# Neighbourhood attention on one Trainium2 core: its operands split where they are made, and its first loads and the decays put in order

## The chip, the core and the metric

The kernel runs on one core of a Trainium2 chip. The metric is the device time of one execution in microseconds (us). TensorE (PE) multiplies matrices, VectorE (DVE), ScalarE (ACT) and GpSimd (POOL) work on tiles in on-chip memory (SBUF, and PSUM for results of matmuls), and SyncE (SP) and POOL issue the transfers (DMAs) between SBUF and DRAM. Each engine runs its own instructions in order and waits on the others by semaphores.

## The reference

One layer of an encoder on 1024 tokens of width 1024: a half-step SwiGLU feed-forward, token mixing, a second feed-forward. Token mixing is what matters here:

```python
rq, rk, rv, rg, nq, nk, nv, g_ret, g_na = jnp.split(u @ w_in, points, axis=-1)
q = _rotary(heads(rq, RET_QK_DIM), pos)
k = _rotary(heads(rk, RET_QK_DIM), pos) * (RET_QK_DIM ** -0.5)
y = _bidirectional_retention(q, k, heads(rv, RET_V_DIM), decay_fwd, decay_bwd)
...
y_na = _neighborhood_attention(na_heads(nq), na_heads(nk), na_heads(nv), rel_bias) @ w_na_out
merged = jax.nn.sigmoid(g_ret) * y_ret + jax.nn.sigmoid(g_na) * y_na
return merged @ w_out
```

Neighbourhood attention has 8 heads of 64 on a grid of 16 rows by 64 columns. A block of 16 query columns looks at 32 key columns and a window of 8 rows:

```python
qg = (q * (DH ** -0.5)).reshape(B, rows, GRID_W, NH, DH)
s = jnp.einsum('bnqhd,brnkhd->bhnqrk', q_r, k_blk).astype(jnp.float32)
s = jnp.where(col_mask[:, :, None, :], s + bias, NEG_INF)
p = jax.nn.softmax(s.reshape(B, NH, ncb, NA_Q_BLOCK_COLS, kr * NA_K_BLOCK_COLS), axis=-1)
o = jnp.einsum('bhnqrk,brnkhd->bnqhd', p, v_blk)
```

## The kernel before

All products are of float32 accuracy made from matmuls in a shorter format. `Core.split` writes a value as a high part h, a rounded copy by ScalarE, and a low part l = value - h, by VectorE (or POOL where the caller asks for it). `mm3` multiplies with three matmuls: high by high, high by low, low by high. The large projections run as Strassen-like block products: `Pairs.run` (one job is two blocks of 512 output columns) loads two weight tiles `wraw` through SP, makes their sums and differences and splits them (`wh`, `wl`), runs seven products, and puts the four halves of the result together on VectorE (L519 to L545). `done(j)` is called as each half is ready.

The mixing projection makes, in order: the first four value tiles (`vproj` with `done_nv`, L1313), four jobs for the queries and keys of neighbourhood attention, after the fourth of them the other four value tiles and the gather, then retention's jobs: rotary ones, in which `rotate` (L1043, L1044) multiplies with sine and cosine tables, stores the half on POOL (L69), and leaves two accumulating DMAs, the swaps (L1048, L1049), for the next `done`; and jobs with an activation (L1374). Finished halves lie in a ring of six tiles, `ev`; a tile can be written again once the DMAs that read it have landed. The halves go to DRAM: `nq`, `nk`, `nv`, `rq`, `rk` and others. The gather (L1387) is four DMAs of SP from DRAM to DRAM that copy the 32 key columns of each of the four column blocks from `nv` into `nvg`, 1 MB each.

`na_cores` (L868) then runs attention as 32 units: 4 pairs of heads, each with 8 pairs of a row group and a column block. A unit's steps: scores by two matmuls a head (L921; each operand of k holds the high part in 64 partitions and the low part in the other 64), bias and row maximum on VectorE (L922, with L924), exponential on ScalarE (L926), reciprocal (L928) and scaling (L930) on VectorE, six transposes on TensorE (L940), a split of these, nine matmuls with the values, and a copy (L956). Steps of three neighbouring units overlap. Before use, the kernel loads keys (`kraw`, L891), queries (`qraw`, L879) and values (`vraw`, L904) from DRAM and splits them: keys on ScalarE and VectorE, or POOL for some, queries with the factor 1/8 (L65, L66), values on ScalarE and VectorE.

Between the steps `fill` takes matmuls from a generator, `products`, which makes the retention values (`vproj` with `done_rv`) and the gates: 12 steps of it ahead of attention, then two and two per unit. `Decays` (L999 to L1035) computes the decay tables of retention from 8 logits by some 45 operations on tiles of 8 columns; it stands in the program at unit 12.

The order in which instructions stand on an engine is set by a scheduler from their dependences, priorities and estimates, so it may differ from the order in which the code is written. DMAs go through eight semaphore lanes on SP and eight on POOL: a DMA waits for the one eight before it.

## Time and profile before

| | us |
|---|---|
| median of three runs | 2256.87 (2256.64 to 2257.74) |
| profiled execution, its own time | 2259.97 |
| its span, first to last instruction | 2258.2 |
| TensorE busy | 2201.1 (97%) |
| VectorE busy | 1638.7 (73%) |
| ScalarE busy | 984.6 (44%) |
| POOL busy | 581.0 (26%) |

Times in the views are us from the start of the span. The query and key jobs run at about 700 to 790, the gather and the rotary jobs from 811 on, attention from about 1005 to 1210. In a timeline a row has the start, the duration, the engine, the line, the operation and its tiles, and in brackets the time that the engine stood idle before and what released it. `PE ps L921 <- ACT qh L65: 2.6, 1, 2.6` in a list of waits reads: TensorE at line 921 waited for the tile qh that ScalarE wrote at line 65, 2.6 us in all, once, the longest 2.6 us.

### The profile page before, as it was taken

The page shows a single profiled execution, that of the slowest core. Times are in us where ns is not written, and L with a number is a line of the kernel's source. Part 1 is how long each engine was busy: PE and PEld are TensorE (multiplying, and loading weights), DVE is VectorE, ACT ScalarE, POOL GpSimd, SP SyncE. Part 2 cuts the span into 40 slices and gives each one's busy share as a digit, 9 for nine tenths or more (in the row PEclk, how much of TensorE's full clock was granted, in tenths as well). Part 3 has the DMA queues.
Part 4 walks back from the last instruction along what each step waited for, and adds up shares of the span by engine and source line. Part 5 has one row for each costly group of instructions (what it writes and reads, how often), then busy time and mean ns, then how long its engine had stood idle before and what let it go on. Part 6 is the DMA issues. An engine that isn't in the chain of part 4 may idle for free. (4 is left out here: it accounts for less than half of the span.)

```text
span 2258.2 us, 30072 instructions
## 1 busy us (share of the span) xinstructions
PE 2201.1 (97%) x10232; PEld 1828.9 (81%) x10232; DVE 1638.7 (73%) x2911; ACT 984.6 (44%) x2039; POOL 581.0 (26%) x755
## 2 busy tenths in 40 slices
PE   7899999999998999999999999999999999999998
PEld 5688888888786887878888888888887888888886
DVE  7998878765558756769885678553899787876444
ACT  5444434332344322248885675422544343433232
POOL 1121212168521122311101222111112121215942
PEclk9999999999999999999999999999999999999999
DMA  6353434598655564557755467686446443449865
GB/s 251 135 188 144 177 131 173 185 386 295 200 173 177 182 177 130 145 181 236 218 179 175 150 220 234 247 306 227 145 145 213 146 170 137 163 153 365 293 225 179
DMA packets 155240, 449.34 MB, mean 199 GB/s; under 512 B 19600, under 2 KB 50448, under 8 KB 152976
## 3 DMA queue, kind: packets, MB, share of 16 engines
q1 hardware_dynamic: 112656, 311.09, 41.1%
q0 software_dynamic: 42432, 136.35, 16.6%
q8 instruction: 81, 1.33, 0.2%
q14 instruction: 71, 0.58, 0.1%
HBM read 302.66 MB, written 148.90 MB: 200 GB/s over the span
## 5 line engine op out<-in xcount | busy, mean ns | idle before, releaser
L63 DVE TENSOR_TENSOR wl<-wraw,wh 128x512 fp32r<-128x512 f32 x472 | 316.9, 688 | 64.9 <-ACT wh L62 64.6
L62 ACT CAST wh<-wraw 128x512 fp32r<-128x512 f32 x476 | 274.6, 618 | 175.3 <-PE ps L90 63.4
L89 PE MATMUL ps<-wh,g 128*128 128x512 f32 x548 | 214.2, 391 | 0.4 <-DVE tmp L226 0.4
L90 PE MATMUL ps<-wl,g 128*128 128x512 f32 x548 | 213.6, 390 | 0.0
L91 PE MATMUL ps<-wh,g 128*128 128x512 f32 x548 | 213.3, 389 | 0.0
L562 ACT ACTIVATE c<-c 128x512 f32<-128x512 f32 x88 | 55.5, 632 | 194.9 <-DVE c L527 101.0
L63 DVE TENSOR_TENSOR wl<-w,wh 128x512 fp32r<-128x512 f32 x77 | 76.9, 1018 | 87.3 <-ACT wh L62 87.1
L63 DVE TENSOR_TENSOR wl<-x,wh 128x512 fp32r<-128x512 f32 x77 | 78.1, 1030 | 77.5 <-ACT wh L62 76.1
L89 PEld LDWEIGHTS ps<-wh,g 128*128 128x128 f32 x548 | 102.9, 188 | 21.8 <-DVE tmp L226 0.7
L90 PEld LDWEIGHTS ps<-wl,g 128*128 128x128 f32 x548 | 102.9, 188 | 21.5 <-DVE wl L63 0.5
L91 PEld LDWEIGHTS ps<-wh,g 128*128 128x128 f32 x548 | 102.9, 188 | 21.4
L89 PE MATMUL ps<-a11h,wh 128*128 128x512 f32 x276 | 111.0, 402 | 7.9 <-ACT wh L62 7.9
L62 ACT CAST wh<-t 128x512 fp32r<-128x512 f32 x58 | 36.0, 621 | 189.0 <-DVE t L521 188.9
L91 PE MATMUL ps<-a11h,wl 128*128 128x512 f32 x276 | 109.4, 397 | 6.3 <-DVE wl L63 6.1
L89 PE MATMUL ps<-a22h,wh 128*128 128x512 f32 x280 | 109.9, 392 | 0.0
L91 PE MATMUL ps<-a22h,wl 128*128 128x512 f32 x280 | 109.2, 390 | 0.6 <-DVE wl L63 0.6
L90 PE MATMUL ps<-a11l,wh 128*128 128x512 f32 x276 | 109.3, 396 | 0.1
L89 PE MATMUL ps<-a12h,wh 128*128 128x512 f32 x276 | 108.8, 394 | 0.5 <-ACT wh L62 0.3
L90 PE MATMUL ps<-a22l,wh 128*128 128x512 f32 x280 | 109.1, 390 | 0.0
L90 PE MATMUL ps<-a12l,wh 128*128 128x512 f32 x276 | 107.5, 390 | 0.0
L91 PE MATMUL ps<-a12h,wl 128*128 128x512 f32 x276 | 107.5, 389 | 0.0
L89 PE MATMUL ps<-s2h,wh 128*128 128x512 f32 x232 | 92.7, 400 | 7.6 <-ACT wh L62 7.6
(430 smaller groups left out, 6295.7 us busy)
## 6 DMA issues: line engine op xcount, KB each, us to landing
wraw<-in_dram SPq DMA_DIRECT2D x204, 512.0 KB, 4.5
g<-g0s SPq DMA_DIRECT2D x44, 512.0 KB, 4.3
g<-g1s SPq DMA_DIRECT2D x44, 512.0 KB, 5.5
g<-g0a SPq DMA_DIRECT2D x33, 512.0 KB, 3.5
g<-g1a SPq DMA_DIRECT2D x33, 512.0 KB, 4.3
g0s<-gth POOLq DMA_DIRECT2D x44, 256.0 KB, 5.0
g0s<-cmb POOLq DMA_DIRECT2D x44, 256.0 KB, 3.8
g1s<-gth POOLq DMA_DIRECT2D x44, 256.0 KB, 4.4
```

What stands on the lines that cost most here:

```text
L62: self.done = [nc.scalar.copy(h, src).ins, (eng or nc.vector).tensor_tensor(l, src, hf, ALU.subtract).ins]
L63: (eng or nc.vector).tensor_tensor(l, src, hf, ALU.subtract).ins]
L89: mm(ps, a[0], b[0], start=start, stop=False)
L90: mm(ps, a[0], b[1], start=False, stop=False)
L91: mm(ps, a[1], b[0], start=False, stop=stop)
L562: nc.scalar.activation(gate[j], gate[j], AF.Silu)
```

## The change

The split of neighbourhood attention's operands moves from `na_cores` to where they are made. In the four jobs `done` splits each half into two tiles (queries, halves 0 and 1, with their columns ordered by column block; keys, halves 2 and 3; the factor 1/8 goes into the keys), and stores both. `done_nv` does so for the values. The DRAM tensors `nq`, `nk`, `nv` and `nvg` have a high and a low part, the gather is eight DMAs, and `na_cores` loads the parts straight into the operands' tiles: 16 DMAs for keys where there were 4, 64 for queries where there were 16, and 32 for values where there were 16. No matmul is added or taken away.

The order is changed in two places. `after` adds order-only dependences: the load of the third fill weight of `vproj` may not stand ahead of attention's first key and query loads (`qk`), and the first three operations of `Decays` may not stand ahead of the reciprocal of the unit last written before it (`c.mark`).

```diff
+    def after(self, e, names):
+        for n in names:
+            self.tc.add_manual_dep(e, n, mybir.DependencyInfo(
+                mybir.DependencyClass.NoSync, mybir.DependencyReason.DATA), reason="order")
...
-def na_cores(c, pool, d, bias, fill, n0, n1, n2, side={}):
+def na_cores(c, pool, d, bias, fill, n0, n1, n2, side={}, first=None):
...
+    def fetch(t, src):
+        names.append(nc.sync.dma_start(t, src).ins.name)
+
+    def qload(hp, cb):
+        q = pool.tile([P, 2, 2, 256], F32, tag="q", name="q", bufs=3)
+        for half in range(2):
+            for n in range(2):
+                fetch(q[64 * half:64 * half + 64, :, n],
+                      d["nq"][hp, n, cb].rearrange("(e p) r c -> p e (r c)", e=2))
+        qop[hp, cb] = [[q[:, e, n].bitcast(F32R) for n in range(2)] for e in range(2)]
...
     def load(hp):
-        kr = pool.tile([P, S], F32, tag="kraw", name="kraw", bufs=1)
-        nc.sync.dma_start(kr, d["nk"][hp])
-        kop[hp] = [pool.tile([P, S], F32R, tag=f"k{e}", name=f"k{e}", bufs=2) for e in range(2)]
...
+            k = pool.tile([P, S], F32, tag=f"k{hp % 2}{e}", name=f"k{hp % 2}{e}", bufs=1)
+            for n in range(2):
+                r = 64 * (e ^ n)
+                fetch(k[r:r + 64], d["nk"][hp, n, 64 * e:64 * e + 64])
+            kop[hp].append(k.bitcast(F32R))
 
     def vload(hp, cb):
...
-        c.split(vh, vl, vr)
-        vop[hp, cb] = vh, vl
+        v = [pool.tile([P, 4, P], F32, tag=f"v{q}", name=f"v{q}", bufs=3) for q in "hl"]
+        for n in range(2):
+            nc.sync.dma_start(v[n], d["nvg"][n, cb][:, :, hp * P:(hp + 1) * P].rearrange("t p d -> p t d"))
...
-        nc.vector.reciprocal(rc, st[:, 4:6])
+        c.mark = nc.vector.reciprocal(rc, st[:, 4:6]).ins.name
...
     load(0)
-    qload(0)
-    qsplit(0, 0)
+    qload(0, 0)
+    first.extend(names)
     fill(n0)
...
-        nc.vector.tensor_scalar(a, x, -1.0, None, ALU.mult)
+        c.after(nc.vector.tensor_scalar(a, x, -1.0, None, ALU.mult).ins, [c.mark])
...
+                    if k > 3 and qk:
+                        c.after(c.fetch, qk)
+                        qk.clear()
...
     def done_nv(t, b):
-        e = evpool[0].tile([P, 512], F32, tag="ev", name="ev", bufs=6 if len(evpool) == 1 else 4)
-        nc.scalar.copy(e, b)
-        c.store(d["nv"][2 * t:2 * t + 2].rearrange("r c d -> (r c) d"), e)
+        h, l = (evpool[0].tile([P, 512], F32, tag="ev", name="ev", bufs=6 if len(evpool) == 1 else 4) for _ in range(2))
+        c.split(h.bitcast(F32R), l.bitcast(F32R), b)
+        for q, e in enumerate((h, l)):
+            c.store(d["nv"][q, 2 * t:2 * t + 2].rearrange("r c d -> (r c) d"), e)
...
             def done(j):
                 h = j % 2
+                if fn == "na":
+                    a, l = parts[j], half() if j < 2 else parts[j]
+                    hi = half()
+                    if j < 2:
+                        c.split(*[q.bitcast(F32R).rearrange("p (b r c) -> p r b c", b=4, r=8) for q in (hi, l)],
+                                a.rearrange("p (r b c) -> p r b c", b=4, r=8))
+                    else:
+                        c.split(hi.bitcast(F32R), l.bitcast(F32R), a, scale=0.125)
+                    for q, e in enumerate((hi, l)):
...
+                            c.store(g[q][:, h * 512:(h + 1) * 512], e)
+                    return
...
                 for cb in range(4):
-                    nc.sync.dma_start(d["nvg"][cb].rearrange("t (r c) d -> (t r) c d", r=4),
-                                      d["nv"][:, KEY_OFF[cb]:KEY_OFF[cb] + 32, :])
+                    for q in range(2):
+                        nc.sync.dma_start(d["nvg"][q, cb].rearrange("t (r c) d -> (t r) c d", r=4),
+                                          d["nv"][q, :, KEY_OFF[cb]:KEY_OFF[cb] + 32, :])
```

How the instructions stand after the change is shown at three places. The first is SP from the gather (`nvg<-nv`) to attention's first loads; `decx`, `dectb` and `decd` are tables of the decays, `bt` the bias, `rg` a part of retention. Before:

```order
L1387 DMA nvg<-nv 16x16384 x4
L73 DMA wraw<-in_dram 128x1024 x21
L999 DMA decx<-in_dram 128x8
L1018 DMA dectb<-in_dram 128x4
L1020 DMA decd<-in_dram 128x256
L73 DMA wraw<-in_dram 128x1024
L1144 DMA rg<-rg 128x2x128 x2
L891 DMA kraw<-nk 128x1024
L879 DMA qraw<-nq 64x1024 x4
```

With the change:

```order
L1408 DMA nvg<-nv 16x16384 x8
L73 DMA wraw<-in_dram 128x1024 x16
L997 DMA decx<-in_dram 128x8
L1016 DMA dectb<-in_dram 128x4
L1018 DMA decd<-in_dram 128x256
L1142 DMA rg<-rg 128x2x128 x2
L881 DMA k_8444<-nk 64x1024 x2
L881 DMA k_8447<-nk 64x1024 x2
L881 DMA q<-nq 64x2x256 x4
L911 DMA bt<-in_dram 128x768
L881 DMA q<-nq 64x2x256 x4
L73 DMA wraw<-in_dram 128x1024
```

The gather has twice the DMAs, and six weight loads (21 and 1 before, 16 now) stand behind the first key and query loads instead of ahead of them.

The second place is TensorE where attention begins: scores (`L921`), fill matmuls of `vproj` (`wh`, `wl` with `a12h` or `a12l`), the first transposes (`L940`). Before, of the first scores:

```order
L90 MATMUL ps<-wl,a12h 128x512
L921 MATMUL ps<-k_8346,qh 128x384
L91 MATMUL ps<-wh,a12l 128x512
L89 MATMUL ps<-wh,a12h 128x512
L90 MATMUL ps<-wl,a12h 128x512
L91 MATMUL ps<-wh,a12l 128x512
L921 MATMUL ps<-k_8346,ql 128x384
L89 MATMUL ps<-wh,a12h 128x512
```

With the change (lines moved by 5 in `mm3`: L94 to L96):

```order
L96 MATMUL ps<-wh,a11l 128x512
L921 MATMUL ps<-k_8444,q 128x384
L921 MATMUL ps<-k_8447,q 128x384
L921 MATMUL ps<-k_8444,q 128x384
L921 MATMUL ps<-k_8447,q 128x384
L921 MATMUL ps<-k_8444,q 128x384 x2
L921 MATMUL ps<-k_8447,q 128x384 x2
L921 MATMUL ps<-k_8444,q 128x384 x2
L940 MATMUL pt<-ident,s 128x128 x5
L94 MATMUL ps<-wh,a12h 128x512 x3
```

The ten score matmuls now stand in one piece, and right behind them the transposes of the first unit's softmax; the fill that stood among the scores comes after.

On ScalarE the first instruction that needs the exponential's table was the decays' (L1004), ahead of attention. It is now the first unit's:

```order
L1394 ACTIVATE ev<-ev 128x512 x4
L926 ACT_TABLE_LOAD
L926 ACTIVATE s,nast<-s,nast 128x384 x2
L62 CAST wh<-wraw 128x512 x2
L62 CAST pth<-pt 128x384
```

The table load has moved from the operations of the decays to the first softmax.

More of the change, by code (lines that the diff above doesn't have):

```diff
@@ L1008, in __init__ @@
         nc.vector.tensor_tensor(w, z, z, ALU.mult)
-        nc.vector.memset(s, 1.0 / 17.0)
+        c.after(nc.vector.memset(s, 1.0 / 17.0).ins, [c.mark])
         for n in (15, 13, 11, 9, 7, 5, 3, 1):
@@ L1321, in done_rv @@
         return f
-    jobs = [(16 + i, 20 + i, d["nq"][i], d["nk"][i], None) for i in range(NHP)]
+    jobs = [(16 + i, 20 + i, d["nq"][i], d["nk"][i], "na") for i in range(NHP)]
     for i in range(RH):
@@ L1366, in done @@
                 h = j % 2
+                if fn == "na":
[7 more added lines that the diff above has]
+                    for q, e in enumerate((hi, l)):
+                        if j < 2:
+                            c.store(f[q][:, :, 8 * h:8 * h + 8].rearrange("b p r c -> p b (r c)"),
+                                    e.rearrange("p (b x) -> p b x", b=4))
+                        else:
+                            c.store(g[q][:, h * 512:(h + 1) * 512], e)
+                    return
                 dst = (f, g)[j // 2][:, h * 512:(h + 1) * 512]
```

44 lines of the change are left out of this document (14 added, 30 removed).

## The prediction

> **What bounds the kernel now.** I read the page first, then one table of windows, then the waits of TensorE, and last the timelines of the three places that the change touches. The page:
>
> ```profile
> span 2258.2 us, 30072 instructions
> ...
> PE 2201.1 (97%) x10232; PEld 1828.9 (81%) x10232; DVE 1638.7 (73%) x2911; ACT 984.6 (44%) x2039; POOL 581.0 (26%) x755
> ...
> PE 38%; DVE 1%; issue 1%; ACT 0%; POOL 0%; DMA 0%; POOLq 0%; DVEq 0%
> ```
>
> TensorE is busy 2201.1 of 2258.2 us, and the chain that ended last runs almost only over it. The change leaves every matmul in place, so it can only move TensorE's idle time. The windows (columns: window, length, busy us and count of PE, PEld, DVE, ACT, POOL, then granted clock, DMA share, GB/s) say where that idle time is:
>
> ```profile
> 700.00:800.00 100.00, 96.03 (x423) 78.51 (x422) 73.50 (x117) 32.64 (x56) 11.61 (x21) 1.00 0.48 161
> 800.00:900.00 100.00, 97.61 (x424) 80.29 (x423) 63.49 (x99) 27.42 (x49) 25.75 (x38) 0.98 0.59 171
> ...
> 1000.00:1100.00 100.00, 93.97 (x517) 80.66 (x516) 88.36 (x260) 81.40 (x207) 13.71 (x17) 0.98 0.78 245
> 1100.00:1200.00 100.00, 99.12 (x576) 87.24 (x575) 75.48 (x215) 76.37 (x197) 6.50 (x12) 1.00 0.59 189
> ```
>
> The first two windows hold the projection that makes queries, keys and values; the others hold the attention. Attention idles TensorE 100 - 93.97 = 6.0 us in its first window and 0.9 in the next, while VectorE is 88% and ScalarE 81% busy. TensorE's waits from 990 to 1130 name what ended them:
>
> ```profile
> PE ps L921 <- ACT qh L65: 2.6, 1, 2.6
> PE ps L89 <- ACT pth L62: 2.0, 2, 1.6
> PE pt L940 <- DVE ptl L63: 1.3, 2, 0.9
> PE pt L940 <- DVE s L930: 1.0, 2, 0.7
> ```
>
> Together 6.9 us: one wait for the first split query, the rest for the softmax and the split of its transposed result. That 6.9 us of idle is the pool from which the attention half can gain. Matmuls that start late without a named wait may add a little, by my estimate 2 us at most, so I bound the gain there at 9.
>
> **Part one, the splits move into the projection (690 to 810).** Four jobs now do four splits each on halves, one ScalarE and one VectorE operation per half, and the value tiles get eight VectorE subtracts. Rows of the projection:
>
> ```profile
> 727.25 0.69 DVE L530 TENSOR_TENSOR ev<-ps,ev 128x512 f32<-128x512 f32 x1 [1.95 <-PE ps L91]
> 729.96 0.69 DVE L534 TENSOR_TENSOR ev<-ps,ev 128x512 f32<-128x512 f32 x1 [2.03 <-PE ps L91]
> 730.57 0.68 DVE L520 TENSOR_TENSOR wraw<-wraw 128x512 f32<-128x512 f32 x1
> ```
> ```profile
> 715.12 0.50 PE L91 MATMUL ps<-a11h,wl 128*128 128x512 f32 x1 [3.34 <-DVE wl L63]
> ```
> ```profile
> L69 POOL DMA_DIRECT2D nq<-ev x8: 542/542/558, 720.2 to 782.6; - x8
> ```
>
> VectorE starts such operations 0.60 us apart when nothing waits (729.96 to 730.57), so the added work is (16 + 8) x 0.60 = 14.4 us. It waits for TensorE at 727.25 and 729.96 by about 2 us each, and the window leaves it 26.5 us idle of 100, so 16 splits (9.6 us) fit behind matmuls from there on. Ahead of that, the first four value subtracts (2.4 us) fall into the stretch that ends in TensorE's 3.34 us wait at 715.12, where VectorE is the late one. If each delayed TensorE by its whole length, the cost would be 2.4; one that only takes the place of the existing wait costs nothing. I take 1.0 us, range 0 to 2.4. POOL gets 8 more stores for queries, 8 for keys and 8 for values at 0.542 us, 13 us spread over a window in which it is busy 11.6 of 100: nothing. ScalarE, 32.6 of 100 busy, hides its part too.
>
> **Part two, the gather of the values (811 to 845).** SP copies the value rows in DRAM to a gathered layout, four copies now, eight after. What one batch does to the transfers is in the DMA view of 811 to 827 (first row: busy tenths in 40 slices of 0.4 us) and of 817.9 to 825.2, and in the timelines of SP, POOL, DVE and PE, with the usual landing of a half-size swap (median 3.9 us) from the DMA view of 805 to 860:
>
> ```profile
> 811.83 2.45 SPq L1387 DMA_DIRECT2D nvg<-nv  x4
> ```
> ```profile
> DMA  1000099900004940000099000000994000000420
> ...
> q1 hardware_dynamic: 128, 4.19, 76.5%
> ...
> rq<-ev POOLq DMA_DIRECT2D x1, 256.0 KB, 10.0
> nvg<-nv SPq DMA_DIRECT2D x4, 9.7
> ```
> ```profile
> q1 hardware_dynamic: 64, 2.10, 86.2%
> q0 software_dynamic: 32, 0.13, 5.2%
> ```
> ```profile
> 827.53 0.89 POOL L1048 DMA_DIRECT2D rq<-ev  x1 [9.73 <-DMA rq<-ev]
> 828.12 1.15 POOL L1049 DMA_DIRECT2D rq<-ev  x1
> ```
> ```profile
> rq<-ev POOLq DMA_DIRECT2D x6, 128.0 KB, 3.9
> ```
> ```profile
> 832.08 0.69 DVE L1043 TENSOR_TENSOR ev<-ev,tab 128x512 f32<-128x512 f32 x1 [2.87 <-DMA rq<-ev]
> 832.69 0.68 DVE L63 TENSOR_TENSOR wl<-wraw,wh 128x512 fp32r<-128x512 f32 x1
> ```
> ```profile
> 836.30 0.39 PE L91 MATMUL ps<-s1h,wl 128*128 128x512 f32 x1
> ```
>
> The bursts of slices stand 8 slices apart, 3.2 us: each copy is one wave over all 16 engines, four end near 825.3. The 256 KB store of the rotary query, on POOL's queue, took 10.0 us, and in the second view only half of it (32 packets, 0.13 MB) got through while two waves ran: its packets squeeze in between waves, two per engine each time. POOL then waits 9.73 us for it before it issues the two accumulating swaps (L1048, L1049; 3.9 us each when nothing is in the way), and VectorE's L1043 at 832.08 waits 2.87 us for those, because it writes into their ring slot.
>
> After the change the eight copies begin about 2 us later, since the last of eight value stores comes later and the ring of six tiles makes the fourth split wait for the first store. They end at 814 + 8 x 3.2 = about 840. The store itself still gets its halves through by about 828. But the swaps, issued there, now stand among four more waves: each is half the store, so it too needs two turns, and two swaps need four turns of 3.2 us. They land near 841 and not before 832. L1043 would start about 9 to 10 us later, and the split behind it on VectorE (832.69) with it; its result is used at 836.30, which leaves 836.30 - 833.37 = 2.9 us of slack. TensorE therefore idles 10 - 2.9 = about 7 us. Range: 0, if the swaps get through as soon as the waves thin, to 9.
>
> The Trainium skill has a rule that speaks against this price: DMA: Bandwidth & Descriptors, section "Queues, rings and completion order", says that each DMA engine takes turns between queue rows a whole packet at a time, and that a packet typically holds some 9 to 17 descriptors, which would put a swap's share of one engine into a single turn. The second view does not agree, since half of the store needed a turn of its own; by the rule the swaps would land near 834 and cost TensorE nothing, which is the first rival below.
>
> **Part three, attention (1000 to 1210).** Removed, from the groups of the two windows on VectorE:
>
> ```profile
> L66 DVE SCALAR_TENSOR_TENSOR ql<-qraw,qh 128x256 fp32r<-128x256 f32 x32 | 14.1, 454 | 0.0
> L63 DVE TENSOR_TENSOR vl<-vraw,vh 128x512 fp32r<-128x512 f32 x16 | 11.0, 689 | 1.4 <-ACT vh L62 1.1
> L63 DVE TENSOR_TENSOR k<-kraw,k 64x512 fp32r<-64x512 f32 x10 | 7.7, 784 | 2.2 <-ACT k L62 2.0
> ```
>
> That is 32.8 us off VectorE and about as much off ScalarE. It is not TensorE's time: only the 6.9 us above can come back. The first wait (2.6, for the query) goes, because queries and keys are now fetched before the third fill weight and need no split. What is late next is the softmax of the first unit, since TensorE's order now has no fill between scores and transposes:
>
> ```profile
> 1000.63 0.39 PE L89 MATMUL ps<-wh,a11h 128*128 128x512 f32 x1
> ...
> 1008.79 0.39 PE L89 MATMUL ps<-wh,a12h 128*128 128x512 f32 x1
> ...
> 1020.87 0.34 PE L921 MATMUL ps<-k,qh 128*128 128x384 f32 x1
> 1021.05 0.34 PE L921 MATMUL ps<-k,ql 128*128 128x384 f32 x1
> ```
> ```profile
> 1003.55 1.28 ACT L1004 ACT_TABLE_LOAD   x1
> ...
> 1020.92 0.61 ACT L926 ACTIVATE s<-s,nast 128x384 f32<-128x384 f32 x1
> ```
> ```profile
> 1019.18 0.55 DVE L922 CUSTOM_DVE_ANT_0 s<-ps,bt 128x384 f32<-128x384 f32 x1
> ...
> 1022.83 0.74 DVE L930 TENSOR_SCALAR s<-s,narc 128x384 f32<-128x384 f32 x2
> ```
>
> The 36 fill matmuls end at 1008.8. Ten score matmuls at 0.18 keep TensorE until 1010.6. The first unit's four end at about 1009.6, VectorE's two reductions at 1010.4, and one small operation follows. The table load, 1.28 us, which the decays' exponential did ahead of attention, now stands behind that wait on ScalarE; two exponentials at 0.6 follow, then the reciprocal (about 0.2) and the first half of the scaling (0.37): 1010.6 + 1.28 + 1.2 + 0.2 + 0.4 = 1013.7. TensorE idles some 3.1 us there. The next five units also stand with less fill between, at about 0.5 each, 2.5 us. So 9 comes off and about 6 comes back: -3 us, range 0 to -9. The decays' 45 small operations, moved behind unit 12, lie where VectorE is 75% busy and TensorE 99%: nothing. Twice the loads and more issues on SP delay nothing that stands behind them as long as transfers keep up (a rival below).
>
> **The sum**: +1.0 + 7 - 3 = +5 us. The profiled execution took 2259.97 with a span of 2258.2, the median of three is 2256.87; the difference is put on the median: about 2262. A change under 0.2% (4.5 us) can't be told from none here.
>
> **The rivals.**
> 1. The gather's delay doesn't reach TensorE: the swaps take one turn each, or come ahead of the last waves. For it: the store's other half landed within 2 us of the last wave. Against: the 10.0 us of the store itself. +1 + 0 - 3 = -2, 2255: the same within the bound.
> 2. Faster: the softmax wait at attention's start does not appear either (VectorE and ScalarE, freed of 33 us each, keep every unit ahead), and the gather is harmless: -9 + 1 = -8, 2249. For it: every wait in that stretch ends on those two engines. Against: the chain of the first unit is latency and not load. It decides once less than 2 of the 6 us come back.
> 3. The gather costs its 7 and attention gives its whole 9: +1 + 7 - 9 = -1, 2256.
> 4. A second resource fills up. In the jobs each 2.4 us of splits exceeds the 2 us leads at 727.25 and 729.96; if nothing else absorbs them, 4 x 2.4 = 9.6 us of which I count 5 to 9. Or the transfers: the loads of keys, queries and values double, 2.1, 4.2 and 4.2 MB by the sizes in the order of SP, some 10 MB on the 43 MB of the two windows (245 and 189 GB/s), at a DMA share of 0.78 already. 2262 + 7 = 2269.
> 5. The change doesn't do what it says, the first loads still come behind weights: the 2.6 stays, +7.6, 2264; I count it with the forecast.
>
> **How the numbers follow.** Forecast with 5: 0.40 (slower 0.30, same 0.10). Rival 1: 0.20 (same 0.15, faster 0.05). Rival 2: 0.17, faster. Rival 3: 0.10 (same 0.09, faster 0.01). Rival 4: 0.13, slower. So faster 0.23, same 0.34, slower 0.43. The likeliest case gives 2262, its own range 2258 to 2266. Eight in ten: down to 2250 takes in rivals 1, 3 and most of 2; up to 2268 half of rival 4.
>
> **What would show it.** Right: VectorE's L1043 near 841 waiting about 10 us for a swap and TensorE idle some 7 us in 836 to 846; no wait of scores for queries; a wait of 3 us at the first transposes for L930; 700 to 800 within 1.5 us of 96.0 busy. Wrong: swaps landing before 836 with the gathers still running, attention above 99 of 100 busy from its start, or projection jobs in which TensorE waits for VectorE's splits.

## The result, and the profile after

The changed kernel takes 2281.08 us (median of four runs, 2278.27 to 2286.04); the kernel before took 2257.3 (median of four) beside it. The ratio is 1.0093, 95% interval 1.0079 to 1.0107: slower by about 21 us (the two medians are 23.8 apart), where 5 were predicted and 2268 was the upper end of the range. First the page and the table of windows (columns as before: window, length, busy us and count of PE, PEld, DVE, ACT, POOL, granted clock, DMA share, GB/s):

```profile
span 2278.5 us, 30109 instructions
...
PE 2208.8 (97%) x10232; PEld 1830.2 (80%) x10232; DVE 1623.2 (71%) x2877; ACT 964.9 (42%) x1991; POOL 588.8 (26%) x773
```
```profile
700.00:800.00 100.00, 95.92 (x412) 76.99 (x411) 84.33 (x135) 42.03 (x72) 26.04 (x41) 0.98 0.63 213
800.00:900.00 100.00, 89.41 (x387) 73.08 (x386) 61.44 (x96) 27.32 (x49) 27.12 (x40) 0.97 0.70 209
1000.00:1100.00 100.00, 92.14 (x472) 77.29 (x471) 57.66 (x171) 52.25 (x134) 5.91 (x11) 0.95 0.89 257
1100.00:1200.00 100.00, 96.96 (x565) 83.86 (x564) 77.56 (x244) 70.42 (x191) 6.46 (x12) 1.00 0.88 273
```

VectorE and ScalarE became lighter in attention, as meant (88.4 to 57.7 and 81.4 to 52.3 in its first window), and TensorE's idle time there grew all the same, from 6.0 to 7.9 and from 0.9 to 3.0. The largest loss of a window is in 800 to 900: busy 97.6 before, 89.4 now. TensorE's busy time grew too, from 2201.1 to 2208.8 us, with the same 10232 matmuls: some of them ran slower.

To see where the time goes, one measure is used for all runs: the lag, the start of the n-th of the 10232 matmuls less the start of the n-th matmul in the trace of before. Every kernel has the same number, so a lag that grows between two points is time lost there, and it takes in waits and slow matmuls alike. The points are named by the time that they have before. Ahead of 701 the code is the same, and what stands there is the scatter of one execution against another. Each row is one execution.

```
lag, us, at     701    830    841    875   1004   1096   1236   2242
after          -0.8    1.9   11.7   10.3   10.3   17.1   19.5   20.0
```

So the jobs (701 to 830) lose 2.7, the gather (830 to 875) 8.4 (9.8 by 841), the first half of attention (1004 to 1096) 6.8 and the second (1096 to 1236) 2.4: 20.3, which is the difference of the spans (2278.5 - 2258.2).

The starts of the matmuls also split each loss in two. Each start less that of the one ahead, less the usual pitch of its shape (the median in the trace of before, 227 ns for 512 columns), is how late it came: over 0.39 us it is called a stall here, the rest are matmuls that start a little late one after the other.

```
us                 stalls, before and now    small delays, before and now
jobs                     4.5    4.7                 0.2    2.7
gather                   2.5   10.9                 1.7    1.7
attention, 1st half      7.0    9.7                 3.3    7.5
attention, 2nd half      1.1    2.5                 1.4    2.4
sum                     15.1   27.8                 6.6   14.3
```

Stalls make 12.7 us of the loss and small delays 7.7, as much as TensorE's busy time grew.

**The gather.** The timelines of POOL, VectorE and TensorE and the DMA view of 815 to 846 (first row in 40 slices of 0.78 us):

```profile
818.63 0.54 POOL L69 DMA_DIRECT2D rq<-ev  x1 [5.07 <-DVE ev L1042]
835.01 0.89 POOL L1046 DMA_DIRECT2D rq<-ev  x1 [15.84 <-DMA rq<-ev]
835.61 1.15 POOL L1047 DMA_DIRECT2D rq<-ev  x1
```
```profile
DMA  3096029009900292009900990099009920069920
...
rq<-ev POOLq DMA_DIRECT2D x1, 256.0 KB, 15.9
rq<-ev POOLq DMA_DIRECT2D x2, 128.0 KB, 9.5
...
nvg<-nv SPq DMA_DIRECT2D x8, 15.4
```
```profile
845.22 0.69 DVE L1041 TENSOR_TENSOR ev<-ev,tab 128x512 f32<-128x512 f32 x1 [8.69 <-DMA rq<-ev]
845.83 0.69 DVE L63 TENSOR_TENSOR wl<-wraw,wh 128x512 fp32r<-128x512 f32 x1
```
```profile
837.98 0.39 PE L95 MATMUL ps<-s1l,wh 128*128 128x512 f32 x1
846.57 0.79 PE L96 MATMUL ps<-s1h,wl 128*128 128x512 f32 x1 [8.20 <-DVE wl L63]
847.16 0.63 PE L94 MATMUL ps<-s1h,wh 128*128 128x512 f32 x1
847.59 0.63 PE L95 MATMUL ps<-s1l,wh 128*128 128x512 f32 x1
...
849.58 0.39 PE L94 MATMUL ps<-s1h,wh 128*128 128x512 f32 x1
849.80 0.39 PE L95 MATMUL ps<-s1l,wh 128*128 128x512 f32 x1
```

The query store took 15.9 us beside the eight waves (10.0 beside four), the swaps behind it 9.5 each. VectorE's multiplication (L1041) waited 8.69 us for a swap (the one ahead of it, at 834.64, had waited 8.13 for the store), the split behind it came at 845.83, and TensorE stood 8.20 us. The matmuls after that start 0.43 us apart until 849.5, then 0.22 again. How POOL's queue (q0) came through is in the DMA views of 825 to 830.5, 831 to 834, 834 to 841.5 (all its queues: q0 is not among them) and 841.5 to 846:

```profile
q0 software_dynamic: 64, 0.26, 13.3%
```
```profile
q0 software_dynamic: 15, 0.00, 0.4%
```
```profile
q1 hardware_dynamic: 64, 2.10, 89.5%
q8 instruction: 1, 0.02, 0.9%
```
```profile
q0 software_dynamic: 240, 0.52, 49.3%
```

The store's data were through by 830.5, in two turns between the waves. Packets of 4 bytes, which follow its data, took a third turn near 833, and the store landed at 834.5. The swaps, issued from 835.0, moved no packet while the next two copies of the gather ran (64 packets, 2.1 MB); theirs started at 842.

**Attention.** Two of TensorE's rows:

```profile
1024.40 1.44 PE L940 MATMUL pt<-ident,s 128*128 128x128 f32 x5 [2.91 <-DVE s L930]
...
1076.64 0.73 PE L94 MATMUL ps<-wh,a21h 128*128 128x512 f32 x2 [2.38 <-ACT wh L62]
```

The first is the foretold wait of the first transposes for the softmax. The second is a fill weight whose split stands on ScalarE behind two exponentials and a split of a transposed result:

```profile
1074.03 0.86 ACT L62 CAST pth<-pt 128x384 fp32r<-128x384 f32 x2 [0.47 <-PE pt L940]
1074.77 0.63 ACT L926 ACTIVATE s<-s,nast 128x384 f32<-128x384 f32 x1
...
1075.38 0.61 ACT L926 ACTIVATE s<-s,nast 128x384 f32<-128x384 f32 x1
...
1075.98 1.65 ACT L62 CAST wh<-wraw 128x512 fp32r<-128x512 f32 x3
```

The stalls of the first half are 3.07, 0.82, 1.00, 2.54, 1.09 and 1.16, 9.7 us; before they were 2.80, 0.91 and 1.73, and three of 0.4 to 0.6, 7.0 us. Ahead of each of the six the last thing to end is an instruction of VectorE or ScalarE. That holds for the second too, a score matmul at 1035.18, whose wait the profile puts down to a load of the bias: ScalarE's copy (L956) ended 0.04 us ahead of it. No score waits for a query any more.

### The profile page after: what moved, and what is told of

Same layout as the page of the kernel before. It is cut to its first block, busy times and chain, and to the rows that moved or that the text cites. A ratio compares the mean times of both kernels' runs of the same rounds, so it can differ in the third digit from the quotient of the medians.

```text
span 2278.5 us, 30109 instructions
## 1 busy us (share of the span) xinstructions
PE 2208.8 (97%) x10232; PEld 1830.2 (80%) x10232; DVE 1623.2 (71%) x2877; ACT 964.9 (42%) x1991; POOL 588.8 (26%) x773
## 5 line engine op out<-in xcount | busy, mean ns | idle before, releaser
L94 PE MATMUL ps<-wh,g 128*128 128x512 f32 x548 | 214.1, 391 | 0.4 <-DVE tmp L231 0.4
L96 PE MATMUL ps<-wh,g 128*128 128x512 f32 x548 | 213.3, 389 | 0.0
L94 PEld LDWEIGHTS ps<-wh,g 128*128 128x128 f32 x548 | 102.9, 188 | 21.8 <-DVE tmp L231 0.7
L96 PEld LDWEIGHTS ps<-wh,g 128*128 128x128 f32 x548 | 102.9, 188 | 21.3
L94 PE MATMUL ps<-a11h,wh 128*128 128x512 f32 x276 | 111.0, 402 | 8.8 <-ACT wh L62 7.6
L96 PE MATMUL ps<-a11h,wl 128*128 128x512 f32 x276 | 108.8, 395 | 3.7 <-DVE wl L63 3.5
L94 PE MATMUL ps<-a22h,wh 128*128 128x512 f32 x280 | 109.9, 392 | 0.0
L96 PE MATMUL ps<-a22h,wl 128*128 128x512 f32 x280 | 109.2, 390 | 0.6 <-DVE wl L63 0.6
L94 PE MATMUL ps<-a12h,wh 128*128 128x512 f32 x276 | 109.0, 395 | 0.3 <-ACT wh L62 0.3
L96 PE MATMUL ps<-a12h,wl 128*128 128x512 f32 x276 | 107.6, 390 | 0.0
L96 PE MATMUL ps<-s1h,wl 128*128 128x512 f32 x232 | 91.1, 393 | 10.1 <-DVE wl L63 10.1
```

The source lines that it names most:

```text
L94: mm(ps, a[0], b[0], start=start, stop=False)
L96: mm(ps, a[1], b[0], start=False, stop=stop)
```

## The experiments

The lag against the trace of before, for all of them:

```
lag, us, at         701    830    841    875   1004   1096   1236   2242
e1_gather_spread    0.6    3.7    3.7    3.6   23.0   28.8   29.6   30.8
e2_decays_early     1.7    5.2   16.4   16.3   16.3   25.4   27.2   25.8
e3_first_loads      3.2    6.0   17.1   17.0   17.0   21.2   22.1   23.2
e4_order_alone      0.1    0.1    0.1    0.1    0.1   -1.9   -0.9   -2.2
e5_half_gather      5.0    7.8    7.8    6.4    6.4   13.0   15.7   15.8
e6_qk_only          2.6    6.7    6.7    5.2    5.2    4.6    4.5    5.1
e7_v_only           0.7    1.8   12.0   10.6   10.6    6.1    7.1    6.5
e8_q_one_row        0.7    3.8   14.8   14.7   14.7   21.1   22.5   23.9
e9_light_loads      4.2    7.3   18.9   18.8   18.8   18.9   18.2   17.9
e10_fine_gather    -0.1    2.5    2.5    6.5    6.5   12.1   15.1   16.7
e11_v_fine          5.1    6.4    6.4    8.6    8.6    3.4    4.3    4.0
e12_more_8          2.0    4.6    4.6    3.1    3.1   -0.0    0.9   -1.1
e12_more_4          3.0    4.6    4.6    3.2    3.2   -0.0    0.8   -0.4
e13_order_late      2.6    4.3    4.3    2.8    2.8    1.9    6.4    5.8
e15_qk_more         1.6    3.1    3.1    1.7    1.7    3.0    9.5   11.8
e17_less           -0.5    2.3   14.1   14.1   14.1   20.8   20.3   20.8
e18_more            0.9    4.7   15.5   14.1   14.1   19.5   27.3   28.2
```

The kernel before was measured again beside each group of runs and took 2259.4 to 2261.9 us there, where it had taken 2257.3 beside the change. So the ratios are what can be compared, and a time that was expected in microseconds goes by its ratio to 2257.3.

### Is it the gather that stalls TensorE at 836?

e1 spreads the eight copies, one per job:

```diff
-                for cb in range(4):
-                    for q in range(2):
-                        nc.sync.dma_start(d["nvg"][q, cb]...
+            if NHP <= i < NHP + 8:
+                q, cb = divmod(i - NHP, 4)
+                e = nc.sync.dma_start(d["nvg"][q, cb]...
+                c.after(e.ins, [c.fetch.name])
```

> The changed kernel with the eight gathers spread over SP's queue: three in one piece where eight were, the others one by one behind the weight loads of the next jobs. Theory (the wait at 836 is the swaps of the rotary jobs standing among the waves of the gather): VectorE's wait for the swap falls from 8.7 us to 3 or less, TensorE's 8.2 us wait behind it goes, with the slow matmuls after it, so about 10 us less: 2270 to 2273. Attention keeps its loss. Rival (the late start of the value stores, ring of six tiles, delays the chain of swaps): the wait stays above 5 us and the time above 2276.

Measured: 2292.07 us, ratio 1.0141 (1.0116 to 1.0165). The stall at 836 is gone (lag 3.7 from 830 to 875), yet 19 us are lost between 875 and 1004, in places that had no stall. The timelines of ScalarE in the change and in e1, at the same place of the program:

```profile
896.45 1.66 ACT L62 CAST wh<-wraw 128x512 fp32r<-128x512 f32 x3 [0.65 <-DVE wraw L545]
898.02 0.62 ACT L1394 ACTIVATE ev<-ev 128x512 f32<-128x512 f32 x1
```
```profile
890.94 0.63 ACT L1394 ACTIVATE ev<-ev 128x512 f32<-128x512 f32 x1 [2.04 <-DVE ev L550]
891.48 0.60 ACT L62 CAST wh<-wraw 128x512 fp32r<-128x512 f32 x1
```

The first weight split of a job now stands behind the last activation of the job before, since the scheduler had put the instructions in another order. TensorE waits at five places there, 12.1 us, each time for a split on ScalarE or VectorE; the rest of the 19 us are small delays. The copies' part is confirmed, the time that was expected is not, and the run shows that an edit of a few DMAs can reorder ScalarE.

e5 therefore leaves the place and issues only four of the eight copies; the low parts of the values are then loaded from the high ones.

```diff
-            nc.sync.dma_start(v[n], d["nvg"][n, cb]...
+            nc.sync.dma_start(v[n], d["nvg"][0, cb]...
...
-                    for q in range(2):
+                    for q in range(1):
```

> The changed kernel with four of its eight gathers: only the high part of the values is gathered, and attention loads it in place of the low part too (the low part is left out, the number and size of attention's loads stay). No engine's order changes but for the four DMAs. Theory (the wait at 836 is swaps among gather waves): VectorE's 8.7 us wait there falls to about 3, TensorE's 8.2 us wait and the slow matmuls behind it go, 9 to 10 us less than the changed kernel: ratio to before 1.004 to 1.007. Rival (the late value stores and the ring): the stall stays above 5 us, ratio 1.008 or more.

Measured: 2273.64 us, 1.0060 (1.0042 to 1.0079). All engines but SP keep their order. VectorE's two multiplications wait less (8.13 and 8.69 in the change), and TensorE does not wait between 815 and 860:

```profile
836.71 0.69 DVE L1041 TENSOR_TENSOR ev<-ev,tab 128x512 f32<-128x512 f32 x1 [4.27 <-DMA rq<-ev]
...
841.67 0.69 DVE L1041 TENSOR_TENSOR ev<-ev,tab 128x512 f32<-128x512 f32 x1 [3.07 <-DMA rq<-ev]
```

The lag stays at 7.8 up to 841: the four added copies are the cause of the stall. e10 keeps all eight and makes only their pieces small, with target rows padded from 512 to 528 columns, so that a copy moves rows of 2 KB in place of runs of 64 KB:

```diff
-"nvg": dt("nvg", [2, 4, 4, P, 512]),
+"nvg": dt("nvg", [2, 4, 4, P, 528]),
...
-                        nc.sync.dma_start(d["nvg"][q, cb]...
+                        nc.sync.dma_start(d["nvg"][q, cb][:, :, :512]...
```

> The changed kernel, with the gathered tensor's rows padded by 16 numbers, so that the eight gathers move rows of 2 KB in place of runs of 64 KB; as many bytes; order of all engines the same. Theory (a swap waits for whole waves of 64 KB runs): the swap's packets pass between rows, VectorE's wait at 836 falls from 8.7 us to 4 or less and TensorE's 8.2 us wait to 0 to 3: ratio 1.005 to 1.007. Rival (the bytes of the gather block the engines, whatever their rows): the wait stays at 7 us or more, ratio 1.009 or more.

Measured: 2274.61 us, 1.0057 (1.0037 to 1.0076), with the order unchanged. The timelines of POOL and VectorE, and the list of TensorE's waits from 815 to 860:

```profile
827.97 0.89 POOL L1046 DMA_DIRECT2D rq<-ev  x1 [8.18 <-DMA rq<-ev]
```
```profile
836.82 0.69 DVE L1041 TENSOR_TENSOR ev<-ev,tab 128x512 f32<-128x512 f32 x1 [7.33 <-DMA rq<-ev]
```
```profile
PE ps L94 <- ACT wh L62: 0.6, 1, 0.6
```

POOL waits for the store half as long and TensorE's 8.2 us at 836 are gone. VectorE's wait for the swap did not fall to 4 as expected, it is 7.33; but it ends 8.4 us earlier, since POOL issues the swaps 7 us earlier, and that is ahead of TensorE's need. Between 841 and 875 a longer stall near 871 and slower matmuls behind it take 4 of them back (lag 2.5 to 6.5). So a store on POOL's queue is held up by the length of the copies' pieces, not by their bytes alone.

### What costs attention 9 us: the two orders of the change?

```diff
e2  -        c.after(nc.vector.tensor_scalar(a, x, -1.0, None, ALU.mult).ins, [c.mark])
    +        nc.vector.tensor_scalar(a, x, -1.0, None, ALU.mult)     (and two more)
e3  -                    if k > 3 and qk:
    -                        c.after(c.fetch, qk)
    -                        qk.clear()
e4  the kernel before, with the after() calls of the change and nothing else
```

> The changed kernel without the order of the decays: their three first operations are free to stand ahead of attention again, and the exponential's table load with them. Theory (the table load stands in the first unit's softmax): TensorE's wait for the first transposes falls from 2.9 us to about 1.6, and the time by 1 to 3 us, to 2278 to 2280. Rival (the decays' 45 small operations in VectorE's way cost as much): 2281 to 2284. Neither theory moves the stall at 836.

> The changed kernel without the order of the first loads: the third and later fill weights are again loaded ahead of the first keys and queries. Theory (no fill stands behind the first scores because its weight comes late): the waits of the first units go, 4 to 6 us less, unless scores now wait for queries: 2275 to 2278. Rival (attention loses over all its length, by transfers or by the order on ScalarE): only 0 to 2 us less, 2279 to 2282, with the waits after 1050 unchanged.

> The kernel before with only the second half of the change, the order of first loads and decays; splits stay in attention. Theory (the order trades the wait for the query, 2.6 us, against a softmax without fill, 3 us): 2256 to 2259. Rival (the order alone makes the loss of attention, about 9 us): 2263 to 2267. Rival (the order is good and the doubled loads make the loss): 2250 to 2254.

Measured: e2 2287.38 us, 1.0120 (1.0097 to 1.0144), attention loses 10.9; e3 2283.99, 1.0100 (1.0076 to 1.0124), it loses 5.1; e4 2260.52, 0.9998 (0.9986 to 1.0010), it gains 1.0. The two orders alone cost nothing, and taking either back does not cure the changed kernel. In e2 the first transposes wait 1.18 in place of 2.91, as the theory had it, but the scores ahead of them now wait 2.62 for VectorE; its ratio is nearest to what the rival gives. e3 gives back 4 in the profile, which its time does not tell apart from the change, and scores wait for queries again (1.0 us).

### Which operands?

e6 splits only queries and keys early, e7 only the values; the rest of each is as before. In short:

```diff
e6  vload, done_nv and the gather as before (one nv, four copies, c.split(vh, vl, vr))
e7  load, qload, qsplit and done for the na jobs as before; the values as changed
```

> Queries and keys split early, values as before (one part, four gathers, split in attention), both orders of the change kept. Theory (gather costs 10, and attention loses because of its doubled loads and its order): no stall at 836; attention loses less than the changed kernel's 9 us, about 5; ratio 1.003 to 1.005. If values' loads are the whole loss of attention: 0.997 to 1.000.

> Values split early, with their eight gathers, queries and keys as before, both orders of the change kept. Theory: the stall at 836 is there in full (about 10 us), attention loses little since only 4 MB of loads are added: ratio 1.003 to 1.006. Rival (the stall needs also the doubled stores of queries and keys): below 1.002.

Measured: e6 2266.77 us, 1.0028 (1.0014 to 1.0042), attention -0.7 where a loss of 5 was expected, no stall at the gather; e7 2269.0, 1.0045 (1.0029 to 1.0060), gather +8.8, attention -3.5. Each half alone gives attention a little back; only both together cost it 9. e11 is e7 with the padded rows of e10:

> Only the values split early (queries and keys as before), both orders of the change, and the gather in rows of 2 KB. Theory: attention keeps the gain of 3.5 us that the kernel with only values showed, and the stall at 836 is gone or below 3 us: ratio 0.998 to 1.001. Rival (the gather's bytes block): ratio 1.003 to 1.005 as without the rows.

Measured: 2263.06 us, 1.0010 (0.9999 to 1.0021); gather +2.2, attention -4.3. It is the best version with any part of the split moved, and no better than the kernel before.

### Pieces, or bytes?

e8 lays the stored queries out so that a load has 64 rows of 4 KB in place of four loads of 1 KB pieces:

```diff
-            for n in range(2):
-                fetch(q[64 * half:64 * half + 64, :, n], d["nq"][hp, n, cb]...
+            fetch(q[64 * half:64 * half + 64], d["nq"][hp, cb])
```

> The changed kernel with the query tensor laid out so that a load of one column block is two DMAs of 64 rows of 4 KB in place of four of 64 x 2 rows of 1 KB; as many bytes, half the DMAs and a quarter of the packets, eight more stores in the jobs; every other engine's order as in the changed kernel. Theory (transfers in attention are late because of their number and small pieces): the share of busy DMA engines in 1000 to 1200 falls from 0.88 to below 0.8, the waits after 1050 go, 3 to 5 us less: ratio 1.007. Rival (attention loses by the order of instructions): share falls, waits stay, ratio 1.009 to 1.010.

Measured: 2284.54 us, 1.0113 (1.0088 to 1.0138). Packets from 1010 to 1200 fell from 36.4 to 30.1 thousand, and attention still loses 7.8; the share of busy DMA engines stayed at 0.89, though both theories had it fall. Their number is not the cause. e9 loads half of each fill weight and of each bias during attention, and uses it twice:

```diff
+            raw = self.raw(src[:, :512], 512)
+            return [self.piece(raw[:, :512]) for b in range(2)]
...
-            nc.sync.dma_start(bts[hp, var], bias[hp, var])
+            nc.sync.dma_start(bts[hp, var][:, 0], bias[hp, var][:, 0])
...
```

> The changed kernel with lighter loads in attention: of each fill weight only the first 512 columns are loaded (used for both halves), of each bias only the first head's (used for both); all else stands, the order of a few instructions in attention moves with the scheduler's estimates. That takes some 12 MB of 51 from attention's transfers, about as many as before the change. Theory A (attention lost 9 us because transfers came late, weights 6.2 us in place of 4.5): its loss falls to 3 us or less, ratio about 1.0065. Theory B (it lost because of the order of instructions on TensorE and ScalarE): loads land sooner and the loss stays above 6 us, ratio 1.008 or more.

Measured: 2275.09 us, 1.0057 (1.0035 to 1.0079); attention -0.6. That looked like proof for the transfers. But the order of TensorE's instructions in attention is another one too, and so are its stalls (2.92, 0.88 and 1.43 us). To have bytes alone, the next runs add stores that nobody waits for: e12 to e4 (16 stores of 512 or 256 KB from a tile that is ready), e13 to e4 with each store held behind one of the retention value stores, e15 so to e6. The edit of e13 and e15:

```diff
-            c.store(d["rv"][t][:, j * 512:(j + 1) * 512], e[:, :512])
+            r = nc.gpsimd.dma_start(d["rv"][t]...).ins.name
+            c.after(nc.gpsimd.dma_start(d["more"][8 * j + t], a21[0]...).ins, [r])
```

> The kernel before with the order half of the change, and 16 more stores of 512 KB (rows of 4 KB, an unused tensor) beside the stores of the retention values, so 8.4 MB more of transfers in attention's first 100 us, and no other instruction moved on any engine but POOL. Theory A (transfers alone make attention late): TensorE's lag over 1004 to 1236, which was -1 us in the kernel with the order alone, rises by 6 us or more: ratio 1.003 or more. Theory B (order of instructions): it stays within 2 us: ratio 0.999 to 1.001.

> The same with 16 stores of 256 KB (rows of 2 KB), 4.2 MB. Theory A: 2 to 5 us more in attention, ratio 1.001 to 1.002. Theory B: no more than 1 us, ratio as the order alone.

> The order half alone, as in the run with 16 stores of 512 KB more, which left early, at about 700, and so told nothing of attention; here each stands behind its store of retention values, at 1010 to 1110. TensorE, VectorE and ScalarE keep their order, two rows of SP change places. Theory A (transfers alone make attention late): TensorE's lag over 1004 to 1236 rises from -1 to 5 us or more, DMA share in 1000 to 1100 above 0.9: ratio 1.002 to 1.005. Theory B (order of instructions): share up, lag within 2 us of the kernel without: 0.999 to 1.001.

> The kernel with only queries and keys split early, whose attention lost nothing (-0.7 us), with 16 stores of 256 KB more behind the stores of the retention values: 4.2 MB, what the split values added on the way to the whole change. Every other engine's order is the same. Theory A (bytes): attention now loses 4 us or more. Theory B (order): within 2 us of -0.7.

Both of e12 say nothing: the stores left near 700, and attention moved by -2.2 and -2.4 where e4 has -1.0 (2258.91 us, 0.9995, and 2260.10 us, 0.9999). In e13 and e15 TensorE, VectorE and ScalarE keep their order, and SP too but for two loads of e13 that change places. e13: 2265.87 us, 1.0032 (1.0020 to 1.0043), attention +3.5 where e4 has -1.0, between the two theories. e15: 2276.68, 1.0075 (1.0056 to 1.0094), attention +7.8 where e6 has -0.7. One place in ScalarE's timeline shows how, first e6, then e15, then TensorE in e15:

```profile
1128.39 0.62 ACT L62 CAST wh<-wraw 128x512 fp32r<-128x512 f32 x1 [2.23 <-DMA wraw<-in_dram]
```
```profile
1131.46 0.62 ACT L62 CAST wh<-wraw 128x512 fp32r<-128x512 f32 x1 [6.20 <-DMA wraw<-in_dram]
```
```profile
1134.79 1.48 PE L942 MATMUL pt<-ident,s 128*128 128x128 f32 x6 [3.31 <-DVE ptl L63]
```

In e15 a fill weight lands later, ScalarE stands in front of its split for 6.20 us, the exponentials and splits of the softmax stand behind, and TensorE waits for these. So bytes can cost attention this much. That they are what costs it in the changed kernel does not follow, and the last two runs ask that, with the order of the change untouched.

### Bytes in the changed kernel itself

e17 sends the full retention value stores out early, from other data, and in their place only 16 KB each; e18 adds the 16 stores of 256 KB.

```diff
e17 +            c.store(d["rv"][t]..., a21[0]...); c.store(d["few"][8 * j + t], e[:, :32])
e18 +            c.after(nc.gpsimd.dma_start(d["more"][8 * j + t], a21[0]...).ins, [r])
```

> The changed kernel with 3.9 MB less to move in attention: of each of the 16 retention value stores (256 KB) only 16 KB goes out there; the full stores go out early, near 700, from other data that is ready then, so the retention values are not the reference's. PE, ACT and SP have the same instructions in the same order as the changed kernel, DVE too but for one early pair. If transfers make attention's loss of 9.2 us: 16 stores of 256 KB added cost 8.5 us elsewhere and 16 of 512 KB cost 4.5, so 2 to 7 us come back here and attention loses 2 to 7. If the order of the instructions makes it: 8 to 10, as before. The jobs near 700 may lose a little to the early stores, up to 2.

> The changed kernel with 16 stores of 256 KB more in attention, each behind a retention value store, so 4.2 MB more to move; PE, DVE, ACT and SP have the same instructions in the same order. If transfers make the loss: attention loses 2 to 8 us more than the 9.2 of the changed kernel, 11 to 17. If the order alone makes it: 9.2, within 1.5.

Measured: e17 2281.88 us, 1.0101 (1.0084 to 1.0119), e18 2287.51, 1.0122 (1.0100 to 1.0144). The windows of the two (e17, e18), and TensorE's timelines (e17, e18):

```profile
1000.00:1110.00 110.00, 102.13 (x521) 85.64 (x520) 64.86 (x201) 57.47 (x146) 6.99 (x13) 0.95 0.83 230
1110.00:1200.00 90.00, 88.96 (x525) 78.09 (x524) 71.44 (x215) 65.31 (x178) 5.37 (x10) 1.00 0.89 266
```
```profile
1000.00:1110.00 110.00, 102.11 (x531) 85.78 (x530) 66.24 (x209) 58.28 (x150) 11.33 (x21) 0.97 0.92 267
1110.00:1200.00 90.00, 83.88 (x477) 71.82 (x477) 63.14 (x186) 57.67 (x158) 9.66 (x18) 0.98 0.92 286
```
```profile
1028.22 1.44 PE L940 MATMUL pt<-ident,s 128*128 128x128 f32 x5 [2.91 <-DVE s L930]
...
1080.34 0.73 PE L94 MATMUL ps<-wh,a21h 128*128 128x512 f32 x2 [2.38 <-ACT wh L62]
```
```profile
1028.23 1.44 PE L940 MATMUL pt<-ident,s 128*128 128x128 f32 x5 [2.91 <-DVE s L930]
...
1079.06 1.22 PE L94 MATMUL ps<-wh,a21h 128*128 128x512 f32 x2 [2.38 <-ACT wh L62]
...
1146.98 0.65 PE L94 MATMUL ps<-wh,a11h 128*128 128x512 f32 x1 [2.60 <-ACT wh L62]
```

The whole times do not tell e17 from the change, whose gather lost 8.4 where that of e17 lost 11.8. Over the whole of attention e17 loses 6.2 and e18 13.2, beside 9.2: by the expected sums that speaks for the transfers. But the two halves of attention answer differently:

```
us lost in           1004 to 1096   1096 to 1236
e17 (fewer bytes)        6.7           -0.5
the change               6.8            2.4
e18 (more bytes)         5.4            7.8
e5 / e8 / e10        6.6/6.4/5.6    2.7/1.4/3.0
e1                       5.8            0.8
```

In the first half the stalls do not move: 3.07, 0.82, 1.00, 2.54, 1.09 and 1.16 us stand at the same matmuls, within 0.02 us, in all seven kernels, whether 230 or 267 GB/s go by. 230 is no more than the kernel before moved in this stretch, with stalls of 7.0 us at other matmuls:

```profile
1000.00:1110.00 110.00, 103.09 (x571) 88.38 (x570) 97.81 (x288) 88.62 (x227) 13.71 (x17) 0.98 0.75 235
```

So bytes do not make these stalls; they come with the order of the instructions, which the seven kernels share in attention. What differs among the seven, 5.4 to 6.8, are the small delays behind the stalls, 6.1 to 7.5 us. In the second half the loss goes with the bytes: in e17 no stall over 0.6 us is left there, in the change 0.92, 0.64 and 0.93, in e18 four, the largest of 2.76 us, for a weight that landed late. But with the bytes of the change the loss there is anything from 0.8 to 3.0. Neither theory alone had it: about 7 of the 9 us go with the order, about 1 to 3 with the transfers.

## Why the prediction failed

| step | predicted, us | measured, us |
|---|---|---|
| jobs | +1.0 (0 to 2.4) | +2.7 |
| gather | +7 (0 to 9) | +8.4 |
| attention | -3 (0 to -9) | +9.2 |
| sum | +5 | +20.3 |

**The premise.** "The change leaves every matmul in place, so it can only move TensorE's idle time" did not hold. Of the 20.3 us, 7.7 are the same matmuls run slower, and the sum had no term for that.

**The jobs.** The splits cost next to nothing: the stalls grew by 0.2, inside the range of 0 to 2.4. The other 2.5 are small delays, and e4 and e13, whose jobs are as before, differ by as much: 0.0 and 1.7 lost there. TensorE is 95.92 of 100 busy in 700 to 800, within the 1.5 that the prediction gave.

**The gather.** The chain was right, that the swaps come late among the copies, VectorE waits for them and TensorE for its split, and so were its sizes: L1041 at 845.22 where 841 was said, waiting 8.69 where 10 was said, TensorE 8.20 where 7 was said. Two links were off, and that the end came out near is in part luck. "The store itself still gets its halves through by about 828" is wrong: its data took until 830.5, it landed at 834.5, and so the swaps were issued 6 us later. And the swaps did not take two turns each among the waves: they took none there, and moved at 842, when the last copy was running out. The first rival, by which the time would have been 2255, falls with this: the swaps took 9.5 us each and did not come ahead of the last waves. By the rule of the Trainium skill that the prediction had set beside it (DMA: Bandwidth & Descriptors, "Queues, rings and completion order") a half-size swap needs one turn. These rows disagree: the store's 64 packets of 4 KB needed two turns, which is two packets on each of 16 engines in a turn, and the swaps got no turn. That shorter pieces cut POOL's wait for the store to 8.18 in e10 agrees with turns between queues. The slow matmuls behind the wait, 1.4 us, were not in the sum; by 875 they no longer show in the lag, because the kernel before has 1.7 us of such delays at 866 and the change 0.2 at the same matmuls.

**Attention**, the step that failed: "So 9 comes off and about 6 comes back". What was to come off did, the wait for the query and the others of before, 8.1 us in both halves. What came back was mis-sized. The first softmax wait was foretold at 3.1 and is 3.07. "The next five units also stand with less fill between, at about 0.5 each, 2.5 us" became 0.82, 1.00, 2.54, 1.09 and 1.16, together 6.6; the largest is a weight split that ScalarE's order had put behind a softmax, which the rows of the order would have shown and which I had not followed past the first transposes. So the stalls of the first half grew by 2.7 where they were to shrink. On top came the small delays, 7.5 us where before they came to 3.3, most of them matmuls at half pace behind the two longest stalls. With this the first half of attention lost 6.8.

"Twice the loads and more issues on SP delay nothing that stands behind them as long as transfers keep up" was the second failure: they did not keep up in the second half, for about 1 to 3 us. That was the fourth rival's transfer half, and its price of 7 was too high for the bytes of this change; e18, with 4.2 MB more, loses 7.8 there.

**The other rivals.** The second and third needed attention to give back its 9; relief of VectorE and ScalarE never gave TensorE more than the 4.3 of e11. The fifth falls: no score waits for a query. The range failed because of attention: with the upper bounds of all three parts, 2.4 + 9 + 0, the sum comes to 11.4, since attention was given no loss except by the fourth rival.

What stays open: why the scheduler's order of the whole change has six stalls in the first half and that of e6 or e7 one or two. Its estimates of the loads take part in it (e9, with lighter loads, got another order), but no run changed the order of the changed kernel's attention alone, with its loads as they are.

## What to carry to other kernels

Work taken off an engine that isn't the bound pays only as much as the waits that end on it, and the reordering which the edit sets off can cost more than that: follow the new order of each engine to the last place where the bound engine's slack was small, not to the first. Bulk copies from DRAM to DRAM with long pieces hold up a small store on another queue; look at what waits for that store before doubling them. A new wait of TensorE can cost more than its length, since matmuls behind it may run slower; give that a term. To tell transfers from order, add or take away stores that nobody waits for, with the order kept.

## What the runs showed of the hardware

Behind a wait TensorE can run at half pace for some microseconds. The windows of the changed kernel around the two longest waits:

```profile
836.00:856.00 20.00, 11.80 (x47) 9.32 (x46) 9.85 (x16) 4.68 (x9) 8.21 (x11) 0.83 0.72 191
1020.00:1030.00 10.00, 6.97 (x22) 5.08 (x21) 5.51 (x19) 5.40 (x12) 0.00 (x0) 0.67 1.11 289
```

The granted clock is 0.83 and 0.67, and matmuls of 512 columns start 0.43 us apart in place of 0.23, for 3 us behind the wait of 8.20 and for 6 behind that of 2.91; the shorter wait had the longer slow stretch. The Trainium skill (TensorE: Matmul & The Clock Gate, "Part 1: The HAM clock gate") gives half the clock after an idle window of about 3.4 us; the pitch agrees, and here a wait of 2.91 us was enough.

How long the slow stretch is does not follow from the wait. Behind the wait of 2.91, the same in nine kernels, the small delays of the next 8 us add up to 3.0 us in the change, 2.1 in e10 and 1.9 in e18. And behind a wait of 2.39 that ends at the same matmul in both kernels, at 866.05 before and at 877.76 with the change, the 4 us that follow were slow before and not with the change (clock 0.61 and 1.00):

```profile
866.00:870.00 4.00, 3.95 (x11) 3.14 (x12) 3.80 (x7) 2.18 (x4) 2.07 (x3) 0.61 0.98 154
```
```profile
877.70:881.70 4.00, 3.94 (x17) 3.06 (x18) 3.79 (x7) 2.46 (x5) 1.91 (x3) 1.00 0.94 158
```

So a difference of 1 to 2 us between two executions can be this alone.

A store of 256 KB took 15.9 us to land beside eight copies of 1 MB with 64 KB pieces, the last turn of it for packets of 4 bytes, and POOL's wait for it fell from 15.84 to 8.18 when the same bytes moved in 2 KB rows.
